# The first feed-forward block's last two plain tiles become an eleventh pair of seven-product blocks, and the seam behind it is rewritten

## The chip, the cores and the metric

The kernel runs on one core of a Trainium2 chip. The metric is the device time of one execution in microseconds (us). Before the change the median of 3 runs is 913.45 us (913.07 to 913.5). The names used below are the profile's: PE is the matrix engine, PEld its weight loads, DVE the vector engine, ACT the scalar engine, POOL the GpSimd engine, SP the engine that issues most of the DMAs. PSUM is the memory of eight banks that PE writes its sums into, SBUF the large on-chip memory.

## What is computed

A transformer layer over 512 tokens of width 1024, all in float32:

```python
x = x + 0.5 * swiglu(rmsnorm(x, ffn1_norm), w_gate, w_up, w_down)      # first block
x = x + token_mixer(rmsnorm(x, mix_norm), w_in, w_out, ...)            # two kinds of attention
x = x + 0.5 * swiglu(rmsnorm(x, ffn2_norm), w_gate, w_up, w_down)      # second block
return rmsnorm(x, final_norm)

def swiglu(x, w_gate, w_up, w_down):
    return (silu(x @ w_gate) * (x @ w_up)) @ w_down                    # hidden width 2816
def rmsnorm(x, g):
    return x * rsqrt(mean(x * x, axis=-1) + 1e-6) * g
```

The change lies in the first block's last matrix product, `@ w_down`, and in the norm that follows it, `rmsnorm(x, mix_norm)`, with the first query and key projections behind that.

## The kernel before

**Products of split numbers.** Every float32 operand is split into a high part (ACT casts it, `high`) and the rest (DVE subtracts, `low`); a product is three matmuls, high by high, high by low, low by high (`mm3`, lines 177 to 180). So each operand costs one ACT and one DVE instruction of 128x512 before PE can use it.

**The hidden layer as tiles and pairs.** The 2816 hidden columns are 22 tiles of 128. Tiles are taken in pairs, and the product of a pair with the down weights, a 2x2 product of blocks, is done with seven block products in place of eight (Strassen's scheme; `a11`, `s3`, ... name the weight side, `b11`, `t3`, ... the activation side). The weight sums `s1` and `s3` are made by DMA (a plain load and an accumulating load that POOL issues), `s2` and `s4` by DVE (`total`), the activation sums by an eleven-step chain on ACT and DVE (`kept`).

**Two groups.** In the first block ("a") the pairs 2 to 10 form a group whose down product (`("t", 0)`, 35 operations) runs in the middle of the gate and up products, and the pairs 12 to 20 a second group (`("t", 1)`) at the end. One operation is one pair in one of the seven products: six matmuls of 512 columns. The seven products of the second group are taken in the order of `LATE_SUMS`. Two banks each hold the sums `w`, `z` and `v`; after each product `block_step` adds the banks into the residual `x` (`into`, the DVE rows of line 574). Tokens lie in four tiles of 128 (tokens 0 to 3 below), the width in two halves: `x[tt]` is the left half of token tile tt, `x[4 + tt]` the right. Tokens 0 and 1 are complete after product `s3`, tokens 2 and 3 get their last part from `s4`, the last product.

**The plain tiles.** Tiles 0 and 1 are in no pair. They are split early on (`activated`), their weights are loaded and split during the second group (`plain_load`, `plain_high`, `plain_low`), and their product is plain: 3 matmuls for each of four token tiles, two halves and two tiles. The half for tokens 0 and 1 stands between the products `s1` and `s3`, that for tokens 2 and 3 in the seam (`plain_mm`), each with a DVE addition into `x` (`plain_add`).

**The seam.** For the following norm each token tile goes through a chain of small steps: sums of squares of both halves (`squared`, ACT, and for the left half `first_sum`, DVE, right behind it), `mean` (DVE, then a square root on ACT), `root_part` (three DVE steps of 128x1), `scaled` (ACT for the left half, DVE for the right). PE then turns the tile (`turn`, eight 128x128 transposes into four PSUM banks, two of the eight column tiles k in one bank), and `gathered` splits what came out, for 256 tokens at a time: ACT writes the high part `xh[k]` (line 1376), DVE the rest `xl[k]` (line 1378). PE then takes the chunks c = 0 to 15 (`early_chunk`): chunk c of the first side (tokens 0 and 1) multiplies column tiles 2c and 2c+1, modulo 8, with the first two query and key weight sets, 12 matmuls of 256 columns.

**Who decides the order.** In this part the order on PE, DVE and ACT is written by hand: inside the block a heap of events (`at`, `put`) sorted by a planned time in units of one operation (`STEP`), in the seam a list (`ev`, `pe`) sorted by a planned time in us. The planned times only sort the instructions. Each engine then takes its own in that order, and an instruction that waits holds back those behind it on its engine. The seam's list is issued after all events of the block.

Of the kernel before, what the change touches and what calls it, by code (L numbers as in the profile page):

```python
# [43 lines left out]
EARLY_SLOTS = {(0, 1): ((2, 24), (3, 25)), (1, 0): ((16, 17), (18, 19)), (1, 1): ((20, 21), (6, 7))}  # L44
PLAIN = 2
# [13 lines left out]
LATE_FRESH = ("a11", "a22", "s3")  # L59
TURNED = {  # L60
    "a": {"plain": PLAIN, "pairs": ((2, 4, 6, 8, 10), (12, 14, 16, 18, 20)),
          "sets": {2: (2, 3, 24, 25, 26, 27, 5), **{j: PAIR_SLOTS[(j - 4) // 2 % 4] for j in range(4, 20, 2)},
                   20: LAST_SET},
          "seven": (LATE_SUMS,) * 2, "fresh": (LATE_FRESH,) * 2,
          "later": ((("t", 0), "a11", 2), (("t", 0), "a11", 3),
                    (("t", 1), "a11", 2), (("t", 1), "a11", 3)),
          "a11": 27,
          "s1": ((8, 9, 10, 11, "raw"), (8, 9, 10, 11, 26)),
          "s3": ((2, *(t[0] for t in PAIR_SLOTS)), (*(t[0] for t in PAIR_SLOTS), 5)),
# [5 lines left out]
                    "a22": ((4.4, 4.2, 3.2, 0.5, 1.5),) * 2,  # L75
                    "a12": ((-2.6, -3.6, -4.6, -5.6, -6.6), (-2.6, -3.6, -4.6, -5.6, -3))}},
    "b": {"plain": 0, "pairs": ((2, 4, 6, 8, 10), (0, 12, 14, 16, 18, 20)),
# [20 lines left out]
LATE_CHAIN = (102.5, 103.4, 103.5, 104, 105, 106, 106.5, 107.5, 109, 113, 121)  # L98
# [6 lines left out]
STEP, TILES_STEP = 1410, 5440  # L105
# [12 lines left out]
def tile_macaron(ctx: ExitStack, tc, xs, xT, wf, wgu1, wst1, wdg1, wqk, wvw, wv, wo, wgu2, wst2,  # L118
# [140 lines left out]
    def ffn(wgu, wst, wdg, n0, n1, norm, early, res, nm, hooks, first=None,  # L259
# [12 lines left out]
        ah, al, due = [None] * JF, [None] * JF, []  # L272
        nx, th, tl = [], [], []

        def activated(j, t):
            h = ah[j] = slot(j, f"ah{nm}{j}", F32R)
            l = al[j] = slot(JF + j, f"al{nm}{j}", F32R)
            A.copy(h[:], t[:])
            V.tensor_tensor(l[:], t[:], h[:].bitcast(F32), op=ALU.subtract)

        def gate(j, pg, pu):
            kept_ = close is not None and j >= plain
# [11 lines left out]
            if kept_:  # L294
                g.setdefault(j // 2 * 2, {})[j % 2] = t1
            else:
                activated(j, t1)
# [56 lines left out]
        ups, up_w, g, plains = {}, {}, {}, []  # L354
# [11 lines left out]
        plain, groups = shape["plain"], shape["pairs"]  # L366
# [4 lines left out]
        for u in units:  # L371
            begin[u] = len(ops)
            for o in ((u[0],),) if u[0] == "P" else shape["seven"][u[1]] if u[0] == "t" else SEVEN:
                if close is not None and (u, o[0]) == (("t", 1), "s3"):
                    for tt in range(2):
                        ops.append((u, ("plain",), tt))
                        starts.append(starts[-1] + TILES_STEP // 2)
                for p in range({"t": len(groups[u[1] % 2]), "P": plain // 2}.get(u[0], 1)):
                    ops.append((u, o, p))
                    starts.append(starts[-1] + (TILES_STEP if u[0] == "P" else STEP))  # L380
# [40 lines left out]
        def source(t):  # L421
            u, o, p = ops[t]
            if u[0] == "P":
                return parts[u, p]
# [23 lines left out]
        def high(t):  # L448
            u, o, p = ops[t]
            if o[0] == "P":  # L450
                w_used[0] += p == 0 and not half
                half.clear()
                shift[0] = 0
                made[t] = w_place()
            elif final is not None and (u, o[0]) == (("t", 1), "s4"):
# [26 lines left out]
        def place(tag, name, dt=F32):  # L482
# [6 lines left out]
            if tag == "bc":  # L489
                return res["bc"][:]  # L490
            if close is not None:
# [12 lines left out]
        def block_load(u, o, p):  # L504
            r = block_rows(u, p)
            if o == "a11":
                n = p
                if close is not None and u[1] == 1 and p == 4:
                    dst = parts["A", u, p] = place(shape["a11"], f"ra{nm}{u[1]}{n}")
                    nc.sync.dma_start(dst, r["a11"])  # L510
                    return
# [64 lines left out]
        def product(t):  # L576
# [4 lines left out]
            if u[0] == "P":  # L581
                tiles_product(t, u[1], p)
                return
# [20 lines left out]
        def tiles_load(u, p):  # L604
            dst = parts[u, p] = wp.tile([P, 1024], F32, tag="raw", name=f"rp{nm}{u[1]}{p}")[:]
            for k in range(2):
                nc.sync.dma_start(dst[:, k * 512:(k + 1) * 512], wdg[p, k, :, u[1] * 512:(u[1] + 1) * 512])

        def tiles_product(t, dh, p):
            h, l = made.pop(t)  # L610
            if p == 0:
                made["P", dh] = [pp.tile([P, S], F32, tag=tag, name=f"pp{dh}{n}", bufs=4 if tag == "mm" else 2)[:]
                                 for n, tag in enumerate((("mm",) * 4, ("s", "s", "t", "t"))[dh])]
            banks = made["P", dh]

            def one(tt, k):
                c, w = slice(tt * P, (tt + 1) * P), slice(k * 512, (k + 1) * 512)
                j = 2 * p + k
                mm3(banks[tt], ah[j][:, c], al[j][:, c], h[:, w], l[:, w], j == 0, j == plain - 1)

            for i in range(8):
                one(*((i % 4, i // 4) if p < plain // 2 - 1 else (i // 2, i % 2)))
            if p == plain // 2 - 1:
                for tt in range(NQ):
                    y = x[4 * dh + tt]
                    put(starts[t] + (tt + 1) * TILES_STEP // 4, stt, y, banks[tt], 0.5, y, ALU.add)

        def block_product(t):
            u, o, p = ops[t]
            ps = groups[u[1]]  # L630
            if o[0] == "plain":
                plains[0](p)
                return
# [30 lines left out]
        def block_step(t, u, o, pw, pz, pv, banks):  # L664

            def into(tt, dh, f):
                y = x[4 * dh + tt]
                late = (0, 0, STEP, 1.65 * STEP)[tt] if close is not None and (u[1], o) == (1, "s3") else 0
                put(t + late, stt, y, banks[tt % 2], f, y, ALU.add)

            for i in range(2):
# [13 lines left out]
                elif o == "a22":  # L685
                    into(i, 1, -0.5)
                else:
# [4 lines left out]
        def bank_tags(u):  # L692


            seq = [v for v in units if v[0] != "P"]
            n = seq.index(u)
# [134 lines left out]
        def pipeline():  # L831
            seen = {}
            for t, (u, o, p) in enumerate(ops):
                if u[0] == "t":
                    block_events(t)
                elif u[0] == "P":
                    at(starts[t] - (8 if p == 0 else 9) * STEP, 1.5, tiles_load, u, p)
                    at(starts[t] - (3 if p == 0 else 4) * STEP, 4.5, high, t)
# [1401 lines left out]
```

## Time and profile before

| | |
|---|---|
| median of 3 runs | 913.45 us (913.07 to 913.5) |
| the profiled execution | 913.15 us |
| its span, first to last instruction | 911.4 us |
| busy PE, DVE, ACT, POOL | 903.7, 733.4, 561.3, 100.4 us |
| instructions on PE | 5772 matmuls |
| the stretch that is rewritten | 313.66 us (first plain matmul) to 339.94 us (first chunk), and the second group before it from about 280 us |

The profile's span begins with the first instruction; the profiled execution's own time has 1.75 us around the span. A row of the timeline gives start, duration, engine, line of the kernel, operation, what is written and read, shape, and in brackets the idle time of the engine before the instruction and what ended it. Durations of neighbouring rows on one engine overlap a little, so the spacing of starts, not the sum of durations, tells what a row costs its engine.

### The profile page before, as it was taken

The numbers are of one execution on the slowest core, as the hardware profiler recorded it, in microseconds if no ns is written. First come the engines' busy times: TensorE is split into PE (matmuls) and PEld (weight loads), VectorE is DVE, ScalarE is ACT, GpSimd is POOL, SyncE is SP. The second block draws the span as 40 slices with busy tenths as digits, with TensorE's granted clock in tenths as the row PEclk, the third lists the DMA queues.
The fourth block names the chain that finished last, engine by engine and source line by source line (L and its number), as shares of the span: only waits on it lengthen the run. The fifth ranks groups of instructions, "written<-read, shape, count | busy, mean of one in ns | idle before, by whom it ended". The sixth has DMA issues, their size and how long they took to land.

```text
span 911.4 us, 16044 instructions
## 1 busy us (share of the span) xinstructions
PE 903.7 (99%) x5772; PEld 816.6 (90%) x5772; DVE 733.4 (80%) x1536; ACT 561.3 (62%) x1192; POOL 100.4 (11%) x125
## 2 busy tenths in 40 slices
PE   9999999999999999999999999999999999999997
PEld 7888998899998889888989778989999889999885
DVE  7798998878888886857865545888888888988886
ACT  7445765466667646656766675656666546666673
POOL 0001102121121100000000000010211112212200
PEclk9999999999999999999999999999999999999999
DMA  7454868587778613333443204374778769778912
GB/s 259 130 155 130 231 195 240 131 207 199 206 184 273 162 47 99 99 109 108 126 116 116 70 24 139 93 180 117 197 189 231 175 162 248 199 194 234 244 39 92
DMA packets 67679, 144.67 MB, mean 159 GB/s; under 512 B 7760, under 2 KB 8272, under 8 KB 67600
## 3 DMA queue, kind: packets, MB, share of 16 engines
q1 hardware_dynamic: 51456, 114.07, 38.2%
q0 software_dynamic: 16144, 29.58, 19.5%
q8 instruction: 45, 0.74, 0.3%
q14 instruction: 34, 0.28, 0.1%
HBM read 138.34 MB, written 2.14 MB: 154 GB/s over the span
## 4 chain that ended last, share of the span: by engine, by line
PE 98%; DVE 1%; ACT 0%; DMA 0%; issue 0%; DVEq 0%; SPq 0%; ACTq 0%
PE pt L178 7%; PE pt L180 7%; PE pt L179 7%; PE pq L178 2%; PE pwo L178 2%; PE pq L179 2%; PE pq L180 2%; PE pk L178 2%; PE pk L180 2%; PE pk L179 2%; PE pwo L179 2%; PE pwo L180 2%; PE pua L178 2%; PE pua L180 2%; PE pua L179 2%; PE pga L178 1%
## 5 line engine op out<-in xcount | busy, mean ns | idle before, releaser
L1733 ACT ACTIVATE pr<-pr,mx 128x128 f32<-128x128 f32 (+3 forms) x64 | 36.0, 563 | 36.7 <-DVE mx L1730 36.4
L574 DVE SCALAR_TENSOR_TENSOR x<-pt,x 128x512 f32<-128x512 f32 x52 | 34.5, 688 | 19.1 <-PE pt L180 11.6
L1730 DVE CUSTOM_DVE_ANT_0 pr<-sc,strip 128x128 f32<-128x128 f32 (+3 forms) x64 | 30.5, 489 | 23.1 <-PE sc L1728 22.6
L410 POOL DMA_DIRECT2D s1bg<-wst_dram x10 | 8.7, 866 | 326.2 <-DVE nxb L984 235.2
L478 DVE TENSOR_TENSOR w<-s2b,w 128x512 fp32r<-128x512 f32 x38 | 26.1, 686 | 8.0 <-ACT w L474 8.0
L474 ACT CAST w<-s2b 128x512 fp32r<-128x512 f32 x38 | 23.6, 621 | 7.7 <-DVE s2b L442 7.7
L474 ACT CAST w<-rab 128x512 fp32r<-128x512 f32 x28 | 17.3, 622 | 17.3 <-DVE rab L437 10.0
L474 ACT CAST w<-raa 128x512 fp32r<-128x512 f32 x31 | 19.0, 621 | 14.4 <-DVE raa L437 7.2
L178 PE MATMUL pwo<-w,mh 128*128 128x512 f32 x64 | 25.9, 404 | 0.0
L179 PE MATMUL pwo<-w,mh 128*128 128x512 f32 x64 | 25.0, 391 | 0.0
L180 PE MATMUL pwo<-w,ml 128*128 128x512 f32 x64 | 25.0, 391 | 0.0
L478 DVE TENSOR_TENSOR w<-s2a,w 128x512 fp32r<-128x512 f32 x30 | 20.6, 686 | 4.4 <-ACT w L474 4.3
L474 ACT CAST w<-s2a 128x512 fp32r<-128x512 f32 x30 | 18.6, 621 | 6.8 <-DVE s2a L442 6.3
L1521 DVE TENSOR_TENSOR w<-raw_qk,w 128x512 fp32r<-128x512 f32 x24 | 16.4, 687 | 7.9 <-ACT w L1517 7.8
L179 PE MATMUL pxgb<-ttb,w 128*128 128x256 f32 x80 | 22.5, 281 | 0.0
L410 POOL DMA_DIRECT2D s1ag<-wst_dram x8 | 7.1, 885 | 124.4 <-DMA s3ag<-wst_dram 47.5
L478 DVE TENSOR_TENSOR w<-raa,w 128x512 fp32r<-128x512 f32 x31 | 20.7, 682 | 0.0
L1727 PE MATMUL sc<-k,q 128*128 128x128 f32 (+3 forms) x64 | 20.5, 322 | 0.0
L1728 PE MATMUL sc<-l,q 128*128 128x128 f32 (+3 forms) x64 | 20.2, 322 | 0.0
L179 PE MATMUL pxub<-ttb,w 128*128 128x256 f32 x72 | 20.2, 281 | 0.0
L478 DVE TENSOR_TENSOR w<-rab,w 128x512 fp32r<-128x512 f32 x28 | 18.8, 686 | 0.0
L179 PE MATMUL pwga<-xl,w 128*128 128x256 f32 x64 | 18.0, 281 | 0.0
(1096 smaller groups left out, 3920.2 us busy)
## 6 DMA issues: line engine op xcount, KB each, us to landing
raw_qk<-wqk_dram SPq DMA_DIRECT2D x12, 512.0 KB, 3.5
raw0bg<-wst_dram SPq DMA_DIRECT2D x10, 512.0 KB, 5.4
raw0bu<-wst_dram SPq DMA_DIRECT2D x9, 512.0 KB, 5.6
raw_gua<-wgu_dram SPq DMA_DIRECT2D x8, 512.0 KB, 3.4
raw0ag<-wst_dram SPq DMA_DIRECT2D x8, 512.0 KB, 5.2
strip<-bias_rows SPq DMA_DIRECT2D x16, 256.0 KB, 3.9
raw_wo<-wo_dram SPq DMA_DIRECT2D x8, 512.0 KB, 3.4
raw0au<-wst_dram SPq DMA_DIRECT2D x7, 512.0 KB, 6.7
```

Of the source, the lines that this page charges most:

```text
L178: T.matmul(po, wh, mh, start=first, stop=False, skip_group_check=on)
L179: T.matmul(po, wh, ml, start=False, stop=False, skip_group_check=on)
L180: T.matmul(po, wl, mh, start=False, stop=last, skip_group_check=on)
L410: nc.gpsimd.dma_start(t[:], b, accum_op=ALU.add)
L474: A.copy(made[t][0], source(t))
L478: V.tensor_tensor(l, source(t), h.bitcast(F32), op=ALU.subtract)
L574: V.scalar_tensor_tensor(o, a, f, b, op0=ALU.mult, op1=op1)
L1521: V.tensor_tensor(l[:, c:c + 512], raw[:, c:c + 512], h[:, c:c + 512].bitcast(F32), op=ALU.subtract)
L1727: T.matmul(ps[:, :w], qs[:, qi], ks[:, :w], start=True, stop=False)
L1728: T.matmul(ps[:, :w], qs[:, qi], ls[:, :w], start=False, stop=True)
L1730: V.tensor_tensor_reduce(out=pi, in0=ps[:, :w], in1=st["b"][m][:, w - 1::-1], op0=ALU.add, op1=ALU.min, scale=1.0, scalar=3.0e38, accum_ou ...
L1733: A.activation(pi, pi, AF.Exp, scale=-1.0, bias=st["mx"][:, m, i:i + 1], accum_out=st["ls"][:, m, i:i + 1])
```

## The change

Tiles 0 and 1 become a pair and the first member of the second group, which now has six pairs: (0, 12, 14, 16, 18, 20). All plain products, their loads, splits and additions go, and so does the early split of the two tiles; their unsplit values stay in two SBUF slots, and the eleven-step chain that the other pairs have is run for them during the next pair's gate and up products (`LATE_CHAIN`, now counted from the end of the first group; the second block's places come out as before). Buffers of the second group are assigned anew. In its sixth product, `s3`, the sums move from `v` to `w`, so that the banks of `v` are free for the turned tokens.

The seam is new. Tokens 0 and 1 are turned inside the last product: `turn(0)` before its fifth operation and `turn(1)` before its sixth. The additions of the right halves of tokens 2 and 3 after `s3` are put off to the planned times 3 and 3.7 operations after it. In the seam the two banks of the last product are added into the left halves of tokens 2 and 3 (`summed`) with their chain, in between the eight `gathered` pairs of tokens 0 and 1, and the first chunk follows the last product at once. Tokens 2 and 3 are turned before chunks 4 and 5 (before: 3 and 5).

```diff
-          "seven": (LATE_SUMS,) * 2, "fresh": (LATE_FRESH,) * 2,
+          "seven": (LATE_SUMS, LAST_SUMS_ORDER), "fresh": (LATE_FRESH,) * 2,
...
-    "a": {"plain": PLAIN, "pairs": ((2, 4, 6, 8, 10), (12, 14, 16, 18, 20)),
+    "a": {"pairs": ((2, 4, 6, 8, 10), (0, 12, 14, 16, 18, 20)),
...
-LATE_CHAIN = (102.5, 103.4, 103.5, 104, 105, 106, 106.5, 107.5, 109, 113, 121)
+LATE_CHAIN = (4.5, 5.4, 5.5, 6, 7, 8, 8.5, 9.5, 11, 15, 23)
...
-            t1 = x[(j - 2, 2 + j)[j > 3]] if kept_ else tp.tile([P, S], F32, tag="ptb", name=f"t1{nm}{j}")
+            t1 = slot(j, f"t1{nm}{j}") if j < 2 else x[(j - 2, 2 + j)[j > 3]]
...
-                late = (0, 0, STEP, 1.65 * STEP)[tt] if close is not None and (u[1], o) == (1, "s3") else 0
+                late = (0, 0, 3 * STEP, 3.7 * STEP)[tt] if close is not None and (u[1], o) == (1, "s3") else 0
...
+                elif close is not None and u[1] == 1:
+                    closing["sums"] = banks
                 else:
                     into(2 + i, 0, 0.5)
...
+    def close(at, begin):
+        last = begin + 36 * STEP
...
             todo += [(last + (0.6 + 0.5 * tt) * STEP, 4, squared, 1, tt),
                      (last + (1.3 + 0.8 * tt) * STEP, 0, mean, tt),
-                     (last + (1.6 + 0.8 * tt) * STEP, 0, root_part, tt)]
+                     (last + (1.6 + 0.8 * tt) * STEP, 0, root_part, tt),
+                     (last + (4.4 + 0.6 * tt) * STEP, 4, squared, 1, 2 + tt),
+                     (last + (4 + tt) * STEP, 3.9, turn, tt)]
...
+        def split(side, highs):
+            for k, t in enumerate(highs):
+                ev(t, gathered, "h", 1, side, k, xts)
+                ev(t + 0.45, gathered, "l", 1, side, k, xts)
+
+        def summed(tt):
+            V.scalar_tensor_tensor(x[tt], closing["sums"][tt % 2], 0.5, x[tt], op0=ALU.mult, op1=ALU.add)
...
+        ev(-1.5, V.tensor_scalar_mul, sm[:, KD:2 * KD], sm[:, KD:2 * KD], 2.0)
+        split(0, (-1.3, -0.9, -0.5, 0.3, 1.0, 1.8, 2.5, 3.2))
+        for tt in range(2):
+            t = (0.0, 0.9)[tt]
+            ev(t, summed, 2 + tt)
+            ev(t + 0.6, squared, 0, 2 + tt)
+            ev(t + 1.4, mean, 2 + tt)
+            ev(t + 1.9, root_part, 2 + tt)
+            for i in range(2):
+                ev(t + 2.6, scaled, i, 2 + tt)
+        for t, low, hf, c in ((4.0, 4.7, 0, 0), (5.2, 5.9, 0, 512), (6.6, 7.3, 1, 0), (7.4, 8.1, 1, 512)):
             ev(t, early_high, 1, hf, c, 512)
             ev(low, early_low, 1, hf, c, 512)
...
-        pe(1.36, plain_mm, 2, (0,))
-        pe(0.8, turn, 0)
-        pe(0.8, turn, 1)
-        split(0, now[0])
-        pe(1.36, plain_mm, 2, (1,))
-        chain(2)
-        pe(1.36, plain_mm, 3, (0,))
-        pe(1.36, plain_mm, 3, (1,))
-        chain(3)
         for c in range(16):
-            if c in (3, 5):
-                pe(0.8, turn, 2 + c // 5)
+            if c in (4, 5):
+                pe(0.8, turn, c - 2)
             if c == 5:
-                split(1, now[0])
+                split(1, [now[0] + 0.1 + 0.42 * k for k in range(KD)])
             pe(1.36, step, c)
```

More of the change, by code (lines that the diff above doesn't have):

```diff
@@ L372, in ffn @@
             begin[u] = len(ops)
[L373 to L378, printed above, removed]
+            for o in shape["seven"][u[1]] if u[0] == "t" else SEVEN:
+                for p in range(len(groups[u[1]]) if u[0] == "t" else 1):
                     ops.append((u, o, p))
-                    starts.append(starts[-1] + (TILES_STEP if u[0] == "P" else STEP))
+                    starts.append(starts[-1] + STEP)
         def rows(u):
@@ L449, in high @@
             u, o, p = ops[t]
[L450 to L455, printed above, removed]
+            if final is not None and (u, o[0]) == (("t", 1), "s4"):
                 made[t] = kept_weights(p)
@@ L602, in product @@
                 pair_step(starts[t + 1], u, o[0], banks)
[L604 to L626, printed above, removed]
         def block_product(t):
@@ L864, in pipeline @@
                 at(starts[t], 4, product, t)
-            if final is not None:
-                kept(0, 0, 0, 0, LATE_CHAIN)
+            kept(0, 0, 0, 0, [begin["t", 0] + 7 * len(groups[0]) + n for n in LATE_CHAIN])
             if bias is not None:
@@ L1413, in chain @@
-        def chain(tt):
-            t = now[0]
-            ev(t - 1.2, plain_add, 0, tt)
-            ev(t - 0.5, squared, 0, tt)
-            ev(t + 0.1, plain_add, 1, tt)
-            ev(t + 0.8, squared, 1, tt)
-            ev(t + 1.6, mean, tt)
-            ev(t + 2.0, root_part, tt)
-            for i in range(2):
-                ev(t + 2.7, scaled, i, tt)
-        def split(side, t):
-            for k in range(KD):
-                ev(t + 0.1 + 0.42 * k, gathered, "h", 1, side, k, ts)
-                ev(t + 0.55 + 0.42 * k, gathered, "l", 1, side, k, ts)
+        def split(side, highs):
+            for k, t in enumerate(highs):
+                ev(t, gathered, "h", 1, side, k, xts)
+                ev(t + 0.45, gathered, "l", 1, side, k, xts)
```

153 lines of the change are left out of this document (41 added, 112 removed), and 14 rows, old and new, of the table TURNED.

## The prediction

> **What bounds the kernel now.** I read the page's first part, then PE's waits, then the timeline from 313 to 346 us engine by engine. The span, and what each engine is busy:
>
> ```profile
> span 911.4 us, 16044 instructions
> PE 903.7 (99%) x5772; PEld 816.6 (90%) x5772; DVE 733.4 (80%) x1536; ACT 561.3 (62%) x1192; POOL 100.4 (11%) x125
> ```
>
> All waits of PE on another engine:
>
> ```profile
> PE warm L1146 <- POOL ones_d L1140: 1.0, 1, 1.0
> PE pga L1191 <- ACT w L1171: 0.2, 1, 0.2
> PE pt L1818 <- ACT ptx L1820: 0.2, 1, 0.2
> ```
>
> PE is the bound and waits 1.4 us in all, nowhere in the part that changes. So the time can fall only by matmuls that go, and rise only by waits that PE does not have today. The timeline of PE at the marks of the rewritten stretch:
>
> ```profile
> 313.66 0.39 PE L178 MATMUL pc<-wx,aha 128*128 128x512 f32 x1
> ...
> 319.10 0.39 PE L178 MATMUL pt<-w,h3a 128*128 128x512 f32 x1
> ...
> 325.90 0.39 PE L178 MATMUL pt<-w,h1a 128*128 128x512 f32 x1
> ...
> 331.34 0.39 PE L178 MATMUL pt<-w,xl 128*128 128x512 f32 x1
> ...
> 334.07 1.91 PE L1411 MATMUL xt<-ident,y 128*128 128x128 f32 x16
> 335.73 0.47 PE L178 MATMUL pc<-wx,aha 128*128 128x512 f32 x1
> ...
> 339.94 0.28 PE L178 MATMUL pq<-xh,wqh 128*128 128x256 f32 x1
> ...
> 344.25 1.03 PE L1411 MATMUL xt<-ident,y 128*128 128x128 f32 x8
> ```
>
> From 313.66 to 319.10 stand 24 plain matmuls, so one takes 0.2267 us of PE and an operation of six 1.36. From 319.10 to 332.70 run `s3` and `s4` (60 matmuls), then 6 plain, 16 transposes (334.07 to 335.73: 1.66 us), 18 plain, and at 339.94 the first chunk. Chunks 0 to 2 take 4.31 us (339.94 to 344.25): 1.44 each, 0.12 a matmul.
>
> **What PE saves.** The stretch 313.66 to 339.94 is 26.28 us. In its place stand 72 matmuls of `s3` and `s4`, 30 more in the five products before (one operation each), and the 16 transposes: 102 x 0.2267 + 1.66 = 24.78. The transposes are now in two places; the matmul after them lasts 0.47 instead of 0.39, so each place costs about 0.08, 0.16 together. 24.94, a saving of **1.34 us**. Turns 2 and 3 stay two separate blocks and cost the same. That is all the change can gain: 0.15%.
>
> **The parts with one answer.** The early split falls away (two casts, two subtractions): 0, PE has no wait there. The chain of pair 0 adds four casts and seven DVE steps between its planned operations 4.5 and 23, about 185 to 212 us:
>
> ```profile
> 185.00:195.00 10.00, 10.00 (x86) 10.00 (x86) 6.49 (x11) 6.30 (x15) 3.51 (x4) 1.00 0.92 227
> 195.00:213.00 18.00, 18.00 (x155) 18.00 (x154) 16.58 (x32) 11.47 (x24) 3.54 (x4) 1.00 0.76 195
> ```
>
> The columns behind the stretch are its length and the busy time of PE, PEld, DVE and ACT. About 2.3 us of DVE and 1.8 of ACT fall into the first stretch, where 3.5 and 3.7 are free; the two late steps of DVE fall into the second, where 1.4 by the sum and more by starts is free, and operands are made three operations (4 us) ahead. 0; without that cover each step would cost PE its 0.6 us. Weights: the pair brings seven issues on SP, two of them followed by an accumulating one on POOL, for four plain loads that go; the first loads of the query weights move from the planned operations 5 and 7 to 9 and 11 of the group, into dead tiles, their casts to 16 to 26. The shortest lead is that of `a11` of the sixth pair, 4.5 operations ahead of the group for a cast one operation into it, 7.5 us:
>
> ```profile
> raw_qk<-wqk_dram SPq DMA_DIRECT2D x12, 512.0 KB, 3.5
> ```
>
> A load of that kind lands in 3.5 us: 0 (bounds: nothing to gain, since PE waits for no load today; above, one late operation, 1.4 us). The splits of operands per operation stay one cast and one subtraction.
>
> **Turns 0 and 1 inside the last product.** T is the start of that product (325.90 in the trace). DVE and ACT behind it, first DVE, then ACT:
>
> ```profile
> 325.42 1.37 DVE L574 SCALAR_TENSOR_TENSOR x<-pt,x 128x512 f32<-128x512 f32 x2
> 326.71 0.68 DVE L478 TENSOR_TENSOR w<-raa,w 128x512 fp32r<-128x512 f32 x1
> ...
> 328.50 0.15 DVE L1382 SCALAR_TENSOR_TENSOR fin<-fin 128x1 f32<-128x1 f32 x1
> ...
> 330.06 0.48 DVE L1341 TENSOR_SCALAR y<-x,fin 128x512 f32<-128x512 f32 x1
> ...
> 331.53 0.49 DVE L1341 TENSOR_SCALAR y<-x,fin 128x512 f32<-128x512 f32 x1
> ```
>
> ```profile
> 326.20 0.63 ACT L1331 ACTIVATE deadh<-x 128x512 f32<-128x512 f32 x1 [0.77 <-DVE x L574]
> 326.74 0.19 ACT L1331 ACTIVATION_READ_ACCUMULATOR deadh<-x 128x1 f32 x1
> 326.96 0.63 ACT L1331 ACTIVATE deadh<-x 128x512 f32<-128x512 f32 x1
> ...
> 328.69 0.20 ACT L1384 ACTIVATE fin<-fin 128x1 f32<-128x1 f32 x1 [1.01 <-DVE fin L1382]
> ...
> 331.53 0.72 ACT L1339 ACTIVATE y<-x,fin 128x512 f32<-128x512 f32 x1 [0.68 <-DVE fin L1390]
> ```
>
> The scaled tiles are there at T+4.64 (330.54) and T+6.35 (332.25). In the new order DVE has the same number of 128x512 steps in this chain (two `into` go behind it, a `total` and a `low` of the sixth pair come in), ACT has one cast more between the two sums of squares: 0.1 later. Turn 0 stands at T + 4 x 1.36 = 5.44, turn 1 at 5.44 + 0.83 + 0.08 + 1.36 = 7.71. Both are ready, with 0.7 and 1.25 us to spare: 0. The last operation ends at T+9.98, and chunk 0 could start there.
>
> **The new seam.** This is where the cover goes: the trace has 18 plain matmuls (4.2 us) between turn 1 and chunk 0, the new order one operation, 1.36. What ACT (first) and DVE do behind the turn today:
>
> ```profile
> 335.36 0.47 ACT L1376 ACTIVATE xh<-xt,x 128x256 fp32r<-128x256 f32 x1 [3.11 <-PE xt L1411]
> 335.73 0.47 ACT L1376 ACTIVATE xh1m<-xt,x 128x256 fp32r<-128x256 f32 x1
> 336.09 0.63 ACT L1331 ACTIVATE sq<-x 128x512 f32<-128x512 f32 x1
> 336.61 0.20 ACT L1331 ACTIVATION_READ_ACCUMULATOR sq<-x 128x1 f32 x1
> ```
>
> ```profile
> 336.23 0.48 DVE L1378 SCALAR_TENSOR_TENSOR xl<-xt,x,xh 128x256 fp32r<-128x256 f32 x1 [1.27 <-ACT xh1m L1376]
> 336.84 0.15 DVE L1248 TENSOR_SCALAR fin<-fin 128x1 f32<-128x1 f32 x1
> 336.91 0.48 DVE L1378 SCALAR_TENSOR_TENSOR xl1m<-xt,x,xh1m 128x256 fp32r<-128x256 f32 x1
> ...
> 340.27 0.47 DVE L1378 SCALAR_TENSOR_TENSOR xl5m<-xt,x,xh5m 128x256 fp32r<-128x256 f32 x1
> 340.66 0.68 DVE L1325 SCALAR_TENSOR_TENSOR x<-pc,x 128x512 f32<-128x512 f32 x1
> 341.26 0.15 DVE L1382 SCALAR_TENSOR_TENSOR fin<-fin 128x1 f32<-128x1 f32 x1
> ...
> 342.45 0.21 DVE L1387 SCALAR_TENSOR_TENSOR fin<-fin 128x1 f32<-128x1 f32 x1
> ...
> 342.97 0.48 DVE L1378 SCALAR_TENSOR_TENSOR xl7m<-xt,x,xh7m 128x256 fp32r<-128x256 f32 x1
> ```
>
> Read from the starts: `xh` costs ACT 0.36, `xl` DVE 0.40, an addition of 128x512 DVE 0.60, `root_part` 0.52, a sum of squares ACT 0.76. Three habits: `xl` of an even tile waits until ACT has done the odd tile of the same bank (336.23 behind 335.73 + 0.47); `first_sum` waits for ACT (336.84 behind 336.61 + 0.20) and holds what is behind it, here `xl1m`; a released instruction starts 0.03 to 0.05 later. I read the first habit both ways: `xh` 3, 5 and 7, which the new list has behind `xl` 2, 4 and 6, wait for these.
>
> Now the new order, from T. The two late `into` of DVE come at 6.12 and 6.76 (behind the last `scaled`), so the sums of squares of tokens 2 and 3 take ACT from 6.85 to 8.37. `xh` 0 and 1 then start at 8.37 and 8.73 (turn 1 would allow 7.71 + 0.46), `xl` 0, 1, 2 at 9.23, 9.63, 10.03, `summed(2)` at 10.43 to 11.12, its squares on ACT 11.15 to 11.90. `first_sum` stands on DVE ahead of `xl` 3 and waits for that: `xl` 3 only at 12.00 to 12.48. `summed(3)` 12.40, `mean`, `xl` 4 at 13.06 to 13.54; the second squares 13.28 to 14.03, `first_sum` waits again; `xh` 5 on ACT is behind the squares, 14.04 to 14.51; `root_part` 14.12; `xl` 5 at 14.64 to 15.12; `mean`, `scaled`, `xh` 6 until 15.80, the second `root_part` until 16.02; `xl` 6 at 16.02 to 16.50, `xh` 7 to 17.01, `xl` 7 at 17.05 to 17.53.
>
> PE asks for column tile k at 9.98 + 0.72 k, for `xl` 0.12 later. Tiles 0 to 2 are in time. Its waits: 0.28 (`xl` 3), 0.34 (`xl` 4), 0.37 and 0.49 (`xh` and `xl` 5), 0.06 and 0.60 (6), 0.31 (`xl` 7): **2.45 us**, in chunks 1 to 3. Chunk 3 ends at 17.59 + 0.60 = 18.19, not 15.74. Turn 2 then finds its tile (ready about 16.4), turn 3 too, and the early casts for chunk 4, queued behind, end about 18.2 on ACT and 18.9 on DVE, before chunk 4 at 19.0.
>
> [...]
>
> Bounds of the waits: if DVE never stood idle from `xl` 0 on, its work up to `xl` 7 is 8 x 0.40 + 2 x 0.60 + 2 x 0.52 + small steps and two `scaled`, 6.6 us; `xl` 7 ends at 15.9 and PE loses 0.8. A gain of more is excluded, since `xl` 0 cannot precede turn 1. Above, each of seven waits may wake PE 0.1 late and the chain may be 0.9 later (below): 3.9. I take 2.45, since every row stands in the trace and the holds are in program order.
>
> **The sum.** -1.34 + 2.45 = +1.1 us (0.12%): slower by less than 0.2%, 1.83 us, which is about what a measurement of this kernel can tell from no change. The profiled execution took 913.15 us (span 911.4 and 1.75 around it), 0.30 under the median of 913.45; it would become 914.25, the median **914.6**.
>
> **The rivals.**
> Gain kept: DVE keeps near its floor and PE loses 0.8 or less: 913.45 - 1.34 + 0.8 = 912.9. For it: DVE's 6.6 us of work fit almost. Against: `first_sum` at 336.84 shows the hold. 14%.
> No effect of the seam at all, the whole 1.34 kept, 912.1: 3%. Even that is within 0.2%.
> Slower: `xl` 0 and `xh` 2 wait for the end of the last operation. Its pair, 20, keeps weights in the tiles of `xl` 0 and `xh` 2 (331.34 reads `xl`), the right halves, while the split writes the left ones. If the order is kept by whole tiles, `xl` 0 starts at 10.1 in place of 9.23, all behind it 0.9 later: +2.0 us, 915.5. It decides as soon as the chain slips by 0.7. Against: DVE writes `w` at 326.71 while PE reads other parts of `w`. 14%.
> Tokens late: if DVE leaves `s3` behind (two additions at 1.29 for both, 325.42 to 326.71, and six `low` and five `total` at 0.60 are 7.9 us of work in 8.2 there), turns and chain slip by the same; from 0.7 us on the result is over the bound, about 915.6. 9%.
> The forecast as it stands has 60%, some of it (4) above the bound. Slower by over 0.2%: 14 + 9 + 4 = 27%, and 3 for what I do not see, 30%; faster by over 0.2% needs more than PE's whole saving, 2%; the rest 68%. The range 912.6 to 916.2 takes in the floor and both slower cases.
>
> **What would show it.** Right: new PE waits on DVE `xl` of about 2.0 us and on ACT `xh` of 0.4 in three chunks, none at the turns; DVE idle ahead of both `first_sum`; from the end of the last operation to turn 2 about 8.2 us, against 5.76 without a wait. Wrong: PE waits on `xl` 0 (whole tiles), at turns 0 or 1 (tokens late), in the second group (queues), or none at all.

## The result and the profile after

The changed kernel took 916.6 us, median of nine runs (915.9 to 919.1); the kernel before took 913.45 in the runs beside it. The ratio is 1.0036, 95% interval 1.0022 to 1.0049: slower by 2.0 to 4.5 us, where 914.6 and a range up to 916.2 had been forecast. The profiled run took 918.43 us, span 916.7. PE is as full as before, only longer (the page's first part):

```profile
span 916.7 us, 16048 instructions
PE 906.6 (99%) x5766; PEld 817.8 (89%) x5766; DVE 733.4 (80%) x1539; ACT 564.5 (62%) x1197; POOL 101.7 (11%) x127
```

PE's waits on other engines. Each row gives the time in all, how often, and the longest wait. Of the three that stood here before, `warm` and `pt` are the same and `pga` has grown from 0.2 to 0.6; the two `pq` rows on DVE are new, and so is `pygb`, in the second block, where no line was edited:

```profile
PE warm L1087 <- POOL ones_d L1081: 1.0, 1, 1.0
PE pq L179 <- DVE xl L1288: 0.8, 2, 0.5
PE pga L1132 <- ACT w L1112: 0.6, 1, 0.6
PE pq L179 <- DVE xl5m L1288: 0.4, 1, 0.4
PE pygb L178 <- ACT pygb L539: 0.3, 1, 0.3
PE pt L1710 <- ACT ptx L1712: 0.2, 1, 0.2
```

This list understates the loss: its `pq` rows come to 1.2 us, while the starts of PE's matmuls show 3.2 in the same place. Those starts are used here. Six rows cut the changed kernel's span into stretches (first matmul into `pyga`; chunk 0; turn 2; first value product `pvw`; first output projection `pwo`; last matmul). The tail is the rest of the span, from the start of the last matmul:

```profile
91.12 0.28 PE L178 MATMUL pyga<-txa,w 128*128 128x256 f32 x1
...
341.46 0.28 PE L178 MATMUL pq<-xh,wqh 128*128 128x256 f32 x1
...
349.52 1.03 PE L1260 MATMUL xt<-ident,y 128*128 128x128 f32 x8
...
369.56 0.45 PE L1476 MATMUL pvw<-w,xh 128*128 128x512 f32 x1
...
524.97 0.48 PE L178 MATMUL pwo<-w,mh 128*128 128x512 f32 x1
...
909.63 0.39 PE L180 MATMUL pt<-kxb,h2b 128*128 128x512 f32 x1
```

The same six marks in every profiled kernel give this table (us; the kernels of its lower rows are described with the experiments):

| kernel | start to `pyga` | to chunk 0 | to turn 2 | to `pvw` | to `pwo` | to last matmul | tail |
|---|---|---|---|---|---|---|---|
| before | 88.41 | 251.53 | 4.31 | 20.82 | 155.41 | 384.20 | 6.67 |
| before_again | 88.76 | 251.51 | 4.31 | 20.61 | 155.40 | 384.22 | 6.68 |
| changed | 91.12 | 250.34 | 8.07 | 20.04 | 155.41 | 384.66 | 7.03 |
| after_again | 88.76 | 250.72 | 8.07 | 20.44 | 155.39 | 384.75 | 7.03 |
| sum_late | 88.90 | 250.31 | 7.25 | 20.33 | 155.40 | 384.20 | 7.04 |
| vw_later | 88.60 | 250.30 | 8.07 | 19.19 | 155.40 | 384.44 | 7.04 |
| behind | 88.78 | 250.38 | 7.18 | 20.00 | 155.42 | 384.22 | 7.03 |
| best | 88.42 | 250.33 | 5.74 | 19.18 | 155.39 | 385.20 | 7.32 |
| best_again | 89.45 | 250.33 | 5.74 | 19.17 | 155.42 | 385.14 | 7.31 |
| best2 | 90.57 | 250.14 | 5.75 | 19.17 | 155.42 | 384.40 | 7.32 |
| best2_again | 88.60 | 250.19 | 5.75 | 19.17 | 155.41 | 384.02 | 7.32 |
| best2_pad | 88.63 | 250.19 | 5.75 | 19.17 | 155.45 | 384.02 | 7.03 |

In the kernel before turn 2 stands behind three chunks (4.31), in all others behind four (5.76 without a wait), so the third and fourth columns are to be read together: 25.13 before, 28.10 changed. The spans of the two profiled executions differ by 5.3 us: 2.71 at the start, -1.19 to chunk 0, +2.97 from chunk 0 to `pvw`, +0.46 in the second block, +0.36 in the tail (together 5.31). The 2.71 is not the change's: the kernel's next profile has 0.35 there.

Inside the seam, DVE and then ACT in the changed kernel (T, the start of the last product, is 331.49 here):

```profile
340.49 0.48 DVE L1288 SCALAR_TENSOR_TENSOR xl<-xt,x,xh 128x256 fp32r<-128x256 f32 x1 [1.60 <-ACT xh1m L1286]
...
343.21 0.15 DVE L1189 TENSOR_SCALAR fin<-fin 128x1 f32<-128x1 f32 x1 [0.85 <-ACT sq L1240]
343.28 0.47 DVE L1288 SCALAR_TENSOR_TENSOR xl3m<-xt,x,xh3m 128x256 fp32r<-128x256 f32 x1
...
345.30 0.15 DVE L1189 TENSOR_SCALAR fin<-fin 128x1 f32<-128x1 f32 x1 [0.49 <-ACT sq L1240]
...
347.27 0.48 DVE L1288 SCALAR_TENSOR_TENSOR xl<-xt,x,xh 128x256 fp32r<-128x256 f32 x1
```

```profile
341.79 0.47 ACT L1286 ACTIVATE xh3m<-xt,x 128x256 fp32r<-128x256 f32 x1 [0.97 <-DVE xl L1288]
...
347.78 0.48 ACT L1286 ACTIVATE xh7m<-xt,x 128x256 fp32r<-128x256 f32 x1
```

`first_sum` (L1189) stands twice, 0.85 and 0.49 us, with `xl` 3 and 5 behind it; `xh` 3 starts when `xl` 2 has ended, and `xh` 7 at 347.78 when `xl` 6 has (347.27 + 0.48). That is the forecast timetable, 0.15 to 0.25 us early.

What was not forecast stands 8 us later, at the first chunk of the second side (tokens 2 and 3, chunk 8). ACT, DVE, SP, POOL and PE:

```profile
355.96 0.62 ACT L1409 CAST w<-raw_vw 128x512 fp32r<-128x512 f32 x1 [3.97 <-DMA raw_vw<-wvw_dram]
356.49 0.47 ACT L1286 ACTIVATE xh<-xt,x 128x256 fp32r<-128x256 f32 x1
```

```profile
350.45 0.69 DVE L1195 TENSOR_TENSOR wql<-raw_q,wqh 128x512 fp32r<-128x512 f32 x1 [0.35 <-ACT wqh L1192]
```

```profile
351.17 0.33 SPq L165 DMA_DIRECT2D raw_vw<-wvw_dram  x1
```

```profile
350.67 0.57 POOL L1355 DMA_DIRECT2D lt<-lams_dram  x1 [44.03 <-ACT wqh L1192]
```

```profile
357.02 0.38 PE L178 MATMUL pq<-xh,wqh 128*128 128x256 f32 x1
...
357.89 0.38 PE L179 MATMUL pq<-xl,wqh 128*128 128x256 f32 x1 [0.50 <-DVE xl L1288]
```

Read backwards: PE waits for the first `xl` of the second side, this for the `xh` that start on ACT at 356.49, and `xh` stands on ACT behind a cast of the wide value weight (`raw_vw`, for the products `pvw` further on), for which ACT has idled 3.97 us. Its load was issued at 351.17, when DVE had ended the subtraction that starts at 350.45 (the last reader of the buffer the load goes to), and landed in 4.8 us. In the kernel before the same cast came almost early enough; SP, POOL, ACT and PE there:

```profile
347.71 0.33 SPq L165 DMA_DIRECT2D raw_vw<-wvw_dram  x1
```

```profile
345.41 0.57 POOL L1463 DMA_DIRECT2D lt<-lams_dram  x1 [40.93 <-ACT sq L1331]
```

```profile
351.46 0.62 ACT L1517 CAST w<-raw_vw 128x512 fp32r<-128x512 f32 x1 [1.54 <-DMA raw_vw<-wvw_dram]
```

```profile
353.17 0.28 PE L178 MATMUL pq<-xh,wqh 128*128 128x256 f32 x1
353.39 0.39 PE L179 MATMUL pq<-xl,wqh 128*128 128x256 f32 x1
353.61 0.28 PE L180 MATMUL pq<-xh,wql 128*128 128x256 f32 x1
```

PE's matmuls of this kind follow each other at 0.12 us; here 0.22 pass, twice, so 0.2 us was lost at this place in this profile too, though the list of waits does not show it. In the next profile of the kernel before nothing was lost.

The load was not late by PE's own clock. In the changed kernel it was issued 1.65 us behind the start of turn 2; in the kernel before 3.46, of which 1.44 are the chunk that stands between, so 2.02. What is longer is its way: 4.8 us to landing in place of 3.7. In the changed kernel a small load that POOL issues (`lt`, 128 KB) goes out 0.50 us ahead of it, in the kernel before 2.30 us. The twelve profiles fall into two groups: with `lt` 0.5 us ahead this load took 4.7 to 5.4 us (changed, after_again, sum_late, vw_later, behind), with `lt` 1.9 to 2.3 us ahead 3.4 to 3.7 (the other seven). No run moves `lt` alone, so that the two loads hinder each other is likely and not shown.

### The profile page after: what moved, and what is told of

Its sections match the earlier page's. It is cut to its first block, busy times and chain, and to the rows that moved or that the text cites. A ratio compares the mean times of both kernels' runs of the same rounds, so it can differ in the third digit from the quotient of the medians.

```text
span 916.7 us, 16048 instructions
## 1 busy us (share of the span) xinstructions
PE 906.6 (99%) x5766; PEld 817.8 (89%) x5766; DVE 733.4 (80%) x1539; ACT 564.5 (62%) x1197; POOL 101.7 (11%) x127
## 4 chain that ended last, share of the span: by engine, by line
PE 93%; DVE 3%; DMA 2%; ACT 2%; issue 1%; SPq 0%; DVEq 0%; ACTq 0%
PE pt L179 7%; PE pt L180 7%; PE pt L178 7%; PE pwo L178 2%; PE pwo L179 2%; PE pwo L180 2%; PE pua L178 2%; PE pua L180 2%; PE pua L179 2%; PE pq L178 1%; PE pq L179 1%; PE pq L180 1%; PE pk L178 1%; PE pk L180 1%; PE pk L179 1%; PE pga L178 1%
## 5 line engine op out<-in xcount | busy, mean ns | idle before, releaser
L453 ACT CAST w<-raa 128x512 fp32r<-128x512 f32 x34 | 21.0, 622 | 17.4 <-DVE raa L421 11.7
L457 DVE TENSOR_TENSOR w<-raa,w 128x512 fp32r<-128x512 f32 x34 | 22.8, 686 | 0.0
L1413 DVE TENSOR_TENSOR w<-raw_qk,w 128x512 fp32r<-128x512 f32 x24 | 16.4, 687 | 7.9 <-ACT w L1409 7.8
```

Of the source, the lines that this page charges most:

```text
L453: A.copy(made[t][0], source(t))
L457: V.tensor_tensor(l, source(t), h.bitcast(F32), op=ALU.subtract)
L1413: V.tensor_tensor(l[:, c:c + 512], raw[:, c:c + 512], h[:, c:c + 512].bitcast(F32), op=ALU.subtract)
```

## The experiments

**Again, unchanged.** Which of the differences belong to the change?

> The changed kernel once more, nothing edited. If its loss is made at the seam: from the end of the last product's last operation to turn 2 again 8.06 us (2.30 more than without a wait), at the first chunk of the second side again 0.74 us of wait, and 0.17 near 208 us; time 915.9 to 916.7. Three other differences of the two traces have no edit beside them: 2.7 us in the first 11 us, 0.45 us near 775 us (second block), 0.4 us behind the last matmul. If they are chance, at least one of them is gone here; if they belong to the change, all stand again with the same size.

Measured: 916.18 us (ratio 1.0036, 1.0023 to 1.0048). Turn 2 at 8.07, and a larger loss at the second side, 1.27 us (20.44 against the 19.17 without a wait) where the first profile had 0.87: the load took 5.2 us. The start took 2.36 us less than in the first profile: chance. The 0.46 of the second block (at 771 and 779 us in the first profile) is gone, but 0.55 us was lost at 859 and 872 us in its place, and 0.34 at 122 us, which no other profile shows. The tail is the same 7.03.

**`first_sum` out of the way** (sum_late): `squares` is `squared` without `first_sum`.

```
-            ev(t + 0.6, squared, 0, 2 + tt)
+            ev(t + 0.6, squares, 2 + tt)
+            ev(t + 1.4, first_sum, 2 + tt)
             ev(t + 1.4, mean, 2 + tt)
```

> One edit: first_sum of tokens 2 and 3 is issued just ahead of mean and no longer right behind the squares; the list of splits stays. Theory (DVE stands at first_sum until ACT has squared, and xl 3, 5, 6, 7 stand behind it): the waits in chunks 1 to 3 fall from 2.30 to about 1.2 us (xl 5 0.25, xl 6 0.65, xl 7 0.3, since xh 5 and 7 still wait for xl 4 and 6 of the same bank), turn 2 comes 6.9 to 7.1 us behind the last operation, the time falls by 1.1 us to about 915.3. Rival (the waits come from the cover that is gone and from the bank order, the place of first_sum is harmless): 2.0 us or more stay, turn 2 at 7.8 or more, time unchanged within 0.3 us.

Measured: turn 2 at 7.25, 0.81 us sooner, so 1.49 of the 2.30 us of waits stay. The saving lies between what the theory (1.1) and the rival (0.3 at most) say. DVE no longer stands at `first_sum`; it now stands for `xh` 5, which ACT has behind the squares. The time did not follow, 916.31 us (ratio 1.003, 1.0018 to 1.0041; its profiled run was the fastest of six, 915.21). The second side waits 1.16 us here (20.33), since the load took 5.1 us; that is no more than in after_again, so why the median did not fall is open. Both waits, DVE's and ACT's:

```profile
342.63 0.48 DVE L1288 SCALAR_TENSOR_TENSOR xl5m<-xt,x,xh5m 128x256 fp32r<-128x256 f32 x1 [0.31 <-ACT xh5m L1286]
```

```profile
353.19 0.62 ACT L1413 CAST w<-raw_vw 128x512 fp32r<-128x512 f32 x1 [4.27 <-DMA raw_vw<-wvw_dram]
```

**The value weight's casts later** (vw_later):

```
-    for n, c in enumerate((3, 5)):
+    for n, c in enumerate((3, 7)):
         put(c, 10, prep, n)
```

> One edit: the two casts of the second wide value weight are issued in steps 7 and 8 and no longer in 5 and 6, so that they do not stand ahead of the casts xh of the second side on ACT. Theory (ACT, in order, waits 4 us for that weight's load, and xh of the second side stand behind it): the wait of 0.74 us at the first chunk of the second side goes, chunks 1 to 3 keep their 2.30; time 0.7 us lower, about 915.9. Rival (xh of the second side are late for another reason: turn 3, or DVE's lows): the wait stays within 0.2 us of 0.74.

Measured: 915.33 us (ratio 1.0019, 1.0007 to 1.0031). Turn 2 at 8.07 as before, and from there 19.19 to `pvw`: the second side's wait is gone, 0.85 us against the first profile of the changed kernel and 1.25 against the second. ACT splits as soon as PE has turned, and waits for the same load behind seven of the eight `xh`, when PE does not yet need the eighth:

```profile
349.70 0.47 ACT L1286 ACTIVATE xh<-xt,x 128x256 fp32r<-128x256 f32 x1 [0.28 <-PE xt L1260]
...
354.06 0.62 ACT L1409 CAST w<-raw_vw 128x512 fp32r<-128x512 f32 x1 [1.69 <-DMA raw_vw<-wvw_dram]
```

So the place of one cast on ACT is the cause, and the slow load only its condition: here the load was issued at 348.61 and was waited for until 354.06, 5.4 us, longer than in the runs above. The six profiles that keep the old place agree on the size. Counted from the start of turn 2 (less 1.44 us in the kernel before), the cast starts at 5.47, 5.77, 6.39, 6.44, 6.73 and 6.85 us, and PE loses 0, 0.2, 0.83, 0.87, 1.16 and 1.27: each tenth of a microsecond behind about 5.6 costs PE the same.

**Splits first, the chain of tokens 2 and 3 behind them** (behind):

```
-        split(0, (-1.3, -0.9, -0.5, 0.3, 1.0, 1.8, 2.5, 3.2))
+        split(0, (-1.3, -0.9, -0.5, -0.1, 0.3, 0.7, 1.1, 1.5))
...
-            t = (0.0, 0.9)[tt]
+            t = (2.0, 2.9)[tt]
```

> The changed kernel with two numbers of the list edited: the eight xh closely behind each other, pair by pair of a bank, and the whole chain of tokens 2 and 3 (additions, squares with first_sum right behind, mean, root, scaled) 2 us later, behind xl 7. Theory (the 1.49 us that were left with first_sum out of the way come from the order: xh 5 and 7 behind xl 4 and 6, squares and additions between the splits): no wait in chunks 1 to 3; the chain, with first_sum still holding DVE twice, is now itself late, and turn 2 waits about 0.85 us: it comes 6.6 us behind the last operation, against 8.06. The casts stay where they are, so the second side waits again 0.8 to 1.3 us. Time 1.4 us under the changed kernel, about 914.8. Rival (xh and xl as such are too much for the cover of one operation): waits of 0.5 us or more stay in chunks 1 to 3.

Measured: 914.9 us (ratio 1.0014, 1.0004 to 1.0023). No wait in chunks 1 to 3: the splits as such fit behind one operation. The second side waits 0.8 (20.00). Turn 2 came at 7.18, 1.42 late where 0.85 was expected. DVE stands idle at `first_sum` twice, 1.7 us in all, and the scaled tile comes after that:

```profile
342.87 0.15 DVE L1189 TENSOR_SCALAR fin<-fin 128x1 f32<-128x1 f32 x1 [0.85 <-ACT sq L1240]
...
344.57 0.15 DVE L1189 TENSOR_SCALAR fin<-fin 128x1 f32<-128x1 f32 x1 [0.88 <-ACT sq L1240]
```

**All three put right** (best): the splits as in behind, `squares` and `first_sum` apart, and vw_later. The list now has the additions between `xl` 3 and 4 and between `xl` 5 and 6, the numbers of tokens 2 and 3 behind `xl` 7, and the first cast for chunk 4 behind `xh` 7.

```
...
+            ev((0.4, 1.2)[tt], summed, 2 + tt)
+            ev((1.7, 2.2)[tt], squares, 2 + tt)
+            ev((2.4, 2.7)[tt], first_sum, 2 + tt)
+            ev((2.4, 2.7)[tt], mean, 2 + tt)
+            ev((2.9, 3.5)[tt], root_part, 2 + tt)
+                ev((3.2, 3.6)[tt], scaled, i, 2 + tt)
...
-        for t, low, hf, c in ((4.0, 4.7, 0, 0), (5.2, 5.9, 0, 512), (6.6, 7.3, 1, 0), (7.4, 8.1, 1, 512)):
+        for t, low, hf, c in ((1.6, 3.3, 0, 0), (5.2, 5.9, 0, 512), (6.6, 7.3, 1, 0), (7.4, 8.1, 1, 512)):
...
```

> Three edits: the eight xh are issued pair by pair of a bank and closely behind each other, the additions of tokens 2 and 3 stand between xl 3 and 4 and between xl 5 and 6, their first_sum, mean and root behind xl 7; the first cast for chunk 4 stands right behind xh 7; the second wide value weight is cast in steps 7 and 8. Theory (the whole loss is order on DVE and ACT, there is time for all of it): DVE works from xl 0 to xl 7 without standing, no wait of PE in chunks 1 to 3 nor at the second side, turn 2 5.76 us behind the last operation; what is left is -1.34 of PE and +0.17 near 208 us: 1.2 us under the kernel before, 912.2 to 912.4 against 913.45. Rival (DVE and ACT have too much work for these chunks whatever the order): 0.8 us or more of waits stay, the time is 913 or above.

Measured: the seam is as expected, turn 2 at 5.74 and 19.18 to `pvw`, no wait anywhere in it. Up to `pwo` PE is 1.43 us ahead of the kernel before (counted from `pyga`). The time is not: 913.19 against 913.46 (ratio 0.9996, 0.9987 to 1.0005), no difference that can be told. In the profile 1.0 us went in the second block, where no line differs, and 0.65 in the tail. A load of `raw0bg` came late; PE's timeline, then ACT's:

```profile
765.84 0.39 PE L178 MATMUL pyub<-xh1m,w 128*128 128x256 f32 x1 [0.46 <-DVE sq L542]
```

```profile
764.10 0.62 ACT L453 CAST w<-raw0bg 128x512 fp32r<-128x512 f32 x1 [2.59 <-DMA raw0bg<-wst_dram]
```

**Chance or not, in the second block**: the two kernels once more.

> The kernel best once more, for its profile. Up to 520 us it was 1.43 us ahead of the kernel before, at the end 0.43: it lost 1.0 us at 766 and 774 us, where ACT and DVE wait for the weights raw0bg. If that is chance of the loads' landing: another loss here (0 to 1 us), at the same places. If being earlier makes it (another load falls in the way): again 0.9 to 1.1 us.

> The kernel before once more, for its profile. If the losses in the second block (766 to 776 us) are chance of the loads: this kernel shows such a loss too in some profile, 0.2 to 1 us against its first one; if they belong to the changed kernels: PE's matmuls stand within 0.05 us of the first profile from 520 us to the end. The wait of 0.20 us at the first chunk of the second side stands again.

Measured (one execution each, 914.35 and 913.25 us): best loses 0.94 us again, at the same places; the kernel before loses nothing again (384.20 and 384.22). Its 0.20 us at the second side, expected to stand again, did not (20.61). By these two pairs alone the loss in the second block would belong to the kernel. But best2, below, has the same second block and the same place in time to 0.2 us (counted from `pyga`), and lost 0.2 in one profile and nothing in the next (384.40, 384.02). What goes with the loss is one load, `raw0bg`, issued near 753 us. The chain of waits of best has it (start, duration):

```profile
752.87 11.15 DMA raw0bg<-wst_dram
```

It landed 11.1 us after its issue in best and best_again, 10.2 in best2 and in the first profile of the kernel before, 9.3 in best2_again, 10.7 in behind and best2_pad, where nothing was lost: only the longest cost a microsecond. What makes it longer in one kernel than in another stays open.

**The added pair's chain** (best2): best, and one step of pair 0's chain moved.

```
-LATE_CHAIN = (4.5, 5.4, 5.5, 6, 7, 8, 8.5, 9.5, 11, 15, 23)
+LATE_CHAIN = (4.5, 5.4, 5.5, 6, 7, 8, 8.5, 9.5, 11, 10.2, 23)
```

In best, DVE had this step ahead of the one that makes `g0a` for another pair:

```profile
202.29 0.69 DVE L706 TENSOR_TENSOR h4a<-t1a,h3a 128x512 fp32r<-128x512 f32 x1
...
203.49 0.42 DVE L548 TENSOR_TENSOR g0a<-g1a,g0a 128x256 f32<-128x256 f32 x1
```

> The edits of the kernel best and one more: the step t0_rest of the added pair 0's chain stands at planned operation 10.2 of its list in place of 15, where DVE had 1.03 us free (195 us). Theory (it stood ahead of g0a's step on DVE, made everything behind it 0.60 late and PE 0.17): the 0.17 us near 206 to 209 us go, and the stretch from the first matmul of the first ungated product (88.4 us) to the first chunk is 1.35 us shorter than in the kernel before, not 1.20; time 0.15 under best. Rival (ACT's casts are what is late there): the 0.17 stay.

> The kernel best2 once more. In five stretches: to the first chunk 250.15 us from the first ungated product, 5.75 to turn 2, 19.17 to the first value product, 155.4 to the output projection, all as in its first profile; in the second block 384.2 to 385.2 (chance of the loads in it) and a tail of 7.35. Time 912.4 to 913.2, 0.3 to 0.9 us under the kernel before. If the second block's 1.0 us of loss in best came from that kernel's place in time, 384.4 again.

Measured: 250.14 and 250.19 us to chunk 0, where best has 250.33 twice: the 0.17 is gone, and it was DVE's. The times are 912.88 against 913.72 (ratio 0.9991, 0.9983 to 1.0000) and, the second time, 912.51 against 913.57 (0.9990, 0.9981 to 0.9998).

**The tail** (best2_pad): best2 with 40 unused copies of one column on ACT and on DVE in the attention part.

```
...
+        if 40 <= t < 80:
+            A.copy(pads[0][:], eps[:])
+            V.tensor_scalar_mul(pads[1][:], eps[:], 1.0)
```

> The kernel best2 with 40 copies of one column on ACT and 40 on DVE, one of each in the planned steps 40 to 79 (attention, about 400 to 470 us), which nothing uses: they only move the engines' later instructions 40 places back in the program. From the last matmul to the end of the span the kernel before takes 6.70 us, the changed one 7.05, best and best2 7.35, with the same instructions; in the last 8 us of the last two kinds one load of instructions (q14) stands that the kernel before does not have there. Theory (where such a load falls is what makes the tail longer): the load leaves the last 8 us, the tail is 6.7 again, 0.65 us less than best2; the copies themselves cost PE at most 0.3. Rival (the tail is longer for another reason): 7.35 stays, with or without the load in it.

Measured: the tail fell from 7.32 to 7.03 us, not to the 6.67 of the kernel before, and no load of instructions is left in the last 8 us. All of the 0.29 is ACT, whose first square of the tail starts 0.77 us behind the start of the last matmul in best2_again (903.14) and 0.48 in best2_pad (903.21):

```profile
903.91 0.60 ACT L1894 ACTIVATE junk<-pt 128x512 f32<-128x512 f32 x1 [1.83 <-PE pt L180]
```

```profile
903.69 0.60 ACT L1899 ACTIVATE junk<-pt 128x512 f32<-128x512 f32 x1 [1.56 <-PE pt L180]
```

So the theory holds for less than half: with the 40 copies this start came 0.29 us sooner. The other 0.36 us above the kernel before stayed without such a load, and the changed kernel has one and no late ACT.

The traces show where the 0.36 goes. The last store lands 5.76 us behind the start of the last matmul in the kernel before and 5.77 in the changed one. Around it SP goes through the program's last waits for semaphores, one every 0.06 us where nothing holds it, twelve in both kernels. The next two lines count those that start ahead of that landing, in the kernel before (up to 910.43 us) and in the changed one (up to 915.38):

```profile
L2236 SPq EVENT_SEMAPHORE  x9: 17/28/28, 908.8 to 909.8; - x9
```

```profile
L2128 SPq EVENT_SEMAPHORE  x3: 17/28/28, 913.8 to 914.8; - x3
```

Six waits that the kernel before passes while its stores are still on the way stand behind the last landing in the changed kernel, and likewise in all ten profiles of edited kernels: 6 x 0.06 = 0.36. This kernel, 912.35 us against 913.57 (ratio 0.9988, 0.9979 to 0.9996), is faster than the kernel before, by 0.4 to 1.9 us.

## Why the prediction was wrong

**What PE saves: right.** 1.34 us forecast. Where the chain of pair 0 is out of the way, the stretch to chunk 0 is 250.14 to 250.19 us against 251.51 and 251.53: 1.32 to 1.39 us less.

**The parts with one answer: 0.17 us too low.** The chain of pair 0 was priced at nothing because DVE had 1.4 us free in the stretch. It was one 0.60 us step in the wrong place, in a stretch where DVE works without a pause (in the changed kernel from 202.02 to 208.50 us no row of DVE has idle time ahead of it). The bound named for a lost cover was 0.6 us a step; 0.17 came of it. best2 removed it. The weights were in time (PE has no wait on the sixth pair in any profile).

**Turns 0 and 1: right.** They start at T + 5.45 and 7.71 (forecast 5.44 and 7.71), and the last operation ends at T + 9.97 (9.98). The two rivals that hung on this place, tokens late and waits by whole tiles, did not happen.

**The seam's first side: right in mechanism and size.** 2.30 us against 2.45. Both holds are in the rows above, and sum_late and behind show them apart: 0.81 us go with `first_sum` moved, and the remaining 1.49 with the splits ahead of the chain. The forecast read its first habit both ways, and that is what shows: `xh` 3 starts on ACT at 341.79 us, 0.04 behind the end of `xl` 2 on DVE (341.28 + 0.47), and `xh` 7 at 347.78, 0.03 behind that of `xl` 6 (347.27 + 0.48); `xh` 5 tells nothing, since the squares hold it until 345.17, longer than `xl` 4 (344.33 + 0.48). The rows show program order between the two readers of a bank, not what would happen without it.

**The step that failed** is the end of the seam: "Turn 2 then finds its tile (ready about 16.4), turn 3 too, and the early casts for chunk 4, queued behind, end about 18.2 on ACT and 18.9 on DVE, before chunk 4 at 19.0." That is true, and there the working stopped: everything behind turn 2 was priced at nothing. ACT has the cast of one more load ahead of the second side's `xh`, with no time to spare already in the kernel before, and the new order sends this load out 0.50 us behind another one; it took 4.8 and 5.2 us to land in place of 3.7 and 3.4. This cost 0.87 us in one profile and 1.27 in the next; the kernel before had 0.2 of it in the profile that the prediction was read from, so +0.66 and +1.06 were missed. vw_later shows the place of the cast as the cause by removing the loss. Why the load took longer is likely the other load, and not shown.

The premise behind the step was the list of PE's waits, "1.4 us in all, nowhere in the part that changes". The starts of PE's matmuls had the 0.2 us there; the list had not.

**What was outside the working.** 0.46 to 0.55 us in the second block and 0.36 in the tail, in code that the change does not touch; the tail's comes with the edited program all the same, from the order of its last waits. With them the sum closes: -1.34 + 0.17 + 2.30 + 0.66 + 0.46 + 0.36 = +2.61, which is what the spans of the two profiled executions differ by without the start. By the profile of after_again it is 3.5 us; the medians, 3.15 apart, lie between. Of the 1.5 us beyond the forecast in the first profile, 0.17 + 0.66 come from chain and seam (the first side took 0.15 less than forecast). That both places had no time to spare could have been read from the profile before; how long the load would take, the 0.46 of the second block, which changes from run to run, and the 0.36 of the tail could not. That the time would rise was forecast for the right reason. The two medians of the changed kernel, 916.6 and 916.18, stand on either side of the range's end, 916.2, so by how much the range was missed is partly chance; the missing step is not.

**The rival "gain kept"** (14%) was the state of things one list away: with the order put right PE loses nothing at all in the seam, below even the 0.8 us taken as the floor. That floor counted the additions and the numbers of tokens 2 and 3 as work ahead of `xl` 7, 6.6 us in all. In best only the two additions stand there, and DVE goes from the start of `xl` 0 to the end of `xl` 7 in 4.4 us (337.79 to 342.20).

## What to carry to other kernels

When a change moves work, follow it past the last wait that you expect: the moved work also decides when buffers come free, when the loads into them go out and which other loads go out beside them, and whatever stands in program order behind the first use of such a load inherits its time to landing (here 4.8 and 5.2 us, with PE held up for 0.87 and 1.27). Look there for places that have no time to spare today, by the starts of the matmuls and not by the list of waits alone (3.2 us against 1.2 here). In a list that an engine takes in order, an instruction that waits for another engine belongs as far back as its reader allows (`first_sum` put off: turn 2 0.81 us sooner in sum_late), and a cast that waits for a load behind the work that others wait for (in vw_later the loss of 0.87 and 1.27 us at the second side is gone). Before blaming an engine's amount of work, try its order: here the same work, listed otherwise, took 3.2 us less from chunk 0 to the value products.

## What the runs showed of the hardware

In some profiles PE starts at about half its later pace: the first real matmuls follow each other at 0.43 us and not 0.227, while the granted clock is shown as 1.00 (the changed kernel's first profile, from 5.4 to 9.8 us at that pace and from 9.8 to 15 us behind it alike). That profile first, then the kernel before:

```profile
6.00 0.63 PE L1132 MATMUL pua<-eha,w 128*128 128x512 f32 x1
6.42 0.63 PE L1132 MATMUL pga<-eha,w 128*128 128x512 f32 x1
```

```profile
5.34 0.40 PE L1191 MATMUL pua<-eha,w 128*128 128x512 f32 x1
5.58 0.39 PE L1191 MATMUL pga<-eha,w 128*128 128x512 f32 x1
```

The last matmul at this pace starts at 9.8 us there, at 8.7 in best2 and at 6.6 in best_again; behind and before_again are slow for the first row or two, and the remaining seven for no more than part of the first row. The warm-up before it is the same (3.66 to 3.79 us), and no edit stands near it; with a first matmul 0.4 us later it makes the 2.7 us by which the starts differ, as much as the whole change cost. The same program had this pace in one profile and not in the next (changed, after_again, where the rows stand 0.23 to 0.24 us apart from the second on); no run shows what sets it.

The profile also lists loads of instructions as a queue of their own, and one of them fell into the last 8 us of all edited kernels but best2_pad, and not into those of the kernel before (q14 in the DMA view). The 40 copies of best2_pad took 0.29 us off the tail; that the load itself was the cause is not shown, and the changed kernel has such a load in the same place without a late ACT.

A load's time to landing is not fixed. The 512 KB load `raw_vw` took 3.4 to 3.7 us in seven profiles and 4.7 to 5.4 in the five where `lt` went out 0.5 us ahead of it; the 512 KB load `raw0bg` took 9.3 us (best2_again) to 11.15 (best) at one place of the second block.
